# One encoder step on one core: seven products for eight in half of the second branch projection, and five modulation blocks summed on TensorE

## The chip, the cores and the metric

The kernel runs on one core of one Trainium2 chip. The metric is the device time of one execution in microseconds. Engines are named as in the profile: PE is TensorE's matmul, PEld its weight load, DVE is VectorE, ACT is ScalarE, POOL is GpSimd, SP is SyncE, which issues nearly all DMAs.

## The reference, cut to what matters

One layer is run for 512 prompt tokens and 64 sample tokens, 576 in all, with a model width of 1024. Two places of it are touched:

```python
mod = (silu(c) @ w_ada + b_ada)             # c: 1024; w_ada: 1024 x 6144, one row per stream
sh1, sc1, gt1, sh2, sc2, gt2 = split(mod, 6)
...
g_attn, g_ssm = split(sigmoid(gate_logits), 2)
mixed = (g_attn * (o_attn @ w_branch_attn) + g_ssm * (y @ w_branch_ssm)) @ w_out
x = x + gt1 * mixed
h2 = rms_normalize(x) * g_norm_ffn * (1 + sc2) + sh2
```

`o_attn` is 576 x 1024, `y` is 576 x 2048, `w_branch_attn` is 1024 x 1024 and `w_branch_ssm` 2048 x 1024. So the second branch projection contracts 16 tiles of 128 channels into 8 tiles of 128 output channels.

## The kernel before

All activations lie channel by channel: 128 channels on the partitions, 576 tokens along the row, and a matmul takes one half of the tokens, 288 columns. Every fp32 product is made of three fp32r matmuls: operands are split into a high part `h` (ACT copies with rounding) and a low part `l` (DVE subtracts), and hh, hl and lh are summed in PSUM. A weight tile is loaded by SP as `raw` (128 x 1024 elements, 512 KB, two buffers), ACT makes `wh` and DVE makes `wl` (three buffers each). `fetch` (line 612) and `getw` (line 641) issue these loads and splits in the order of a list `specs` of weight tiles. `fm` (line 926) makes one output tile: for each of its k tiles, three kinds of matmul times two token halves.

The order of instructions is fixed ahead of the run. The program records operations, and a planner (`Plan.order`, line 391) places them one engine at a time: whichever operation is ready by its own costs goes first, and among ready ones that with the lowest priority number, which is the place in the program less an offset set by `R.prio(...)` (4000 is urgent, -2000 is filler). `R.slack = 3.0` makes the planner place a matmul 3 us after its operands are due. At run time each engine runs its list in order and waits on semaphores only.

The stage in question, in order:

- The last state-space groups are finished beside the first branch projection. Eight tiles `fm(f"pba{a}", ...)` (line 1552) contract `oh`, `ol` (eight tiles each, pool `op_`, line 1316); the result times its gate goes to DRAM as `m_d`.
- `y`'s 16 tiles come from DRAM (`stage<-y_d`, two are kept in SBUF) and are split into `yh`, `yl` (line 1566, pool `yhl`, which opens once the state-space pool has closed).
- Five of the twelve blocks of 512 modulation values (u = 5 to 9; they hold `gt1`, `sh2` and `sc2`) are computed by `ada_columns` (line 770) as fillers: four 512 KB loads of `w_ada` each into two buffers `adr`, and on DVE sixteen multiply-adds of 128 x 512 into two accumulators `aacc`. `ada_sum` (line 787) then sums them over the partitions on PE: eight fp32 matmuls with 32 output rows each, four of them at four column positions of the array, and `ada_out` transposes the result.
- The second branch projection (line 1579): eight tiles of 16 x 3 x 2 matmuls, each then multiplied by its gate, added to `m` and split into `mh`, `ml`.
- The output projection with `w_out`, then the FFN, whose gate, up and down projections already take seven products for eight in part.

Two other ways of getting modulation values stand in the kernel: `ada_pair` at the start, which uses PE for the whole contraction, and `ada` (line 722), which is defined and not called.

Of the kernel before, what the change touches and what calls it, by code (L numbers as in the profile page):

```python
# [5 lines left out]
F32 = mybir.dt.float32  # L6
# [7 lines left out]
P = 128  # L14
# [526 lines left out]
def build(tc, I, O):  # L541
# [57 lines left out]
    queue = []  # L599
    state = {"ld": 0, "sp": 0, "get": 0}  # L600
    raws, outs, outs_made = {}, {}, []

    def fm_spec(w, c0, r0=0):
        specs.append([(kview(w[r0:r0 + 8 * P, c0:c0 + P]), 8, P)])
# [4 lines left out]
    def misc_spec():  # L609
        specs.append(["misc"])  # L610

    def fetch(done, limit=1 << 30):

        while len(outs_made) < len(specs):
            i = len(outs_made)
            outs_made.append(i)
            queue.extend((i, s) for s in specs[i])
            outs[i] = []
        with R.prio(4000 if done or limit > 99 else 0):
            more = True  # L620
            while more:
                more = False
                j = state["ld"]
                if j < min(len(queue), limit) and j < state["sp"] + NRAW:
                    i, s = queue[j]
                    if s == "misc":
                        raw = wp.tile([P, 8, 104], F32, name="rawm", tag="raw", bufs=NRAW)
                        sync.dma_start(raw[:, :, 0:72], kview(w_in[:, C_KI:C_KI + 72]))
                        sync.dma_start(raw[:, :, 72:104], kview(w_in[:, C_DT:C_DT + 32]))
                        raws[j] = (raw, 8, 104)  # L630
                    else:
                        raws[j] = (load_raw(*s), s[1], s[2], 27 <= j < 48)
                    state["ld"] += 1
                    more = True
                j = state["sp"]
                if j < min(state["ld"], limit) and (j < NWH or queue[j - NWH][0] < done):
                    outs[queue[j][0]].append(split(*raws.pop(j)))
                    state["sp"] += 1
                    more = True

    def getw(n=1):
        i = state["get"]
# [39 lines left out]
        nf += 1  # L682
    for a in range(8):
        fm_spec(I["w_branch_attn"][0], P * a)
    for a in range(8):
        fm_spec(I["w_branch_ssm"][0], P * a, 0)
        fm_spec(I["w_branch_ssm"][0], P * a, 1024)

    for a in range(8):
        fm_spec(I["w_out"][0], P * a)  # L690
# [28 lines left out]
    modc = cp.tile([P, 6, 8, 2], F32, name="modc")  # L719
    sh1, sc1, gt1, sh2, sc2, gt2 = (modc[:, i] for i in range(6))  # L720

    def ada(u, pl, bufs):

        p = px(f"pada{u}", "py")
        raws = [pl.tile([P, 2, 512], F32, name=f"wada{u}_{k2}", tag="adr", bufs=bufs) for k2 in range(4)]
        loads = [sync.dma_start(raw, w_ada[256 * k2:256 * k2 + 256, 512 * u:512 * u + 512].rearrange("(k p) n -> p k n", p=P))
                 for k2, raw in enumerate(raws)]
        with R.after(loads[-1:]):
            for kt in range(8):
                for g in range(4):  # L730
                    pe.matmul(p[32 * g:32 * g + 32, 0:P], sil[:, kt, :], raws[kt // 2][:, kt % 2, P * g:P * g + P],
                              start=(kt == 0), stop=(kt == 7), tile_position=(0, 32 * g))
        ada_out(u, p)

    pairs_bank = px("padp", "py")

# [33 lines left out]
    def ada_columns(u, pl, nacc=1, bufs=2, nk=2, tags=None, late=False):  # L770

        acc = [pl.tile([P, 512], F32, name=f"aacc{u}{s}", tag=tags[s] if tags else f"aacc{s}", bufs=nacc) for s in range(2)]
        for k0 in range(0, 8, nk):
            raw = pl.tile([P, nk, 512], F32, name=f"wada{u}_{k0}", tag=tags[2 + k0 // nk % 2] if tags else "adr", bufs=bufs)
            (pool if u == 10 else sync).dma_start(raw, w_ada[P * k0:P * (k0 + nk), 512 * u:512 * u + 512].rearrange("(k p) n -> p k n", p=P))
            for j in range(nk):
                kt = k0 + j
                for s in range(2):
                    if kt == 0:
                        vec.tensor_scalar(acc[s], raw[:, j], sil[:, kt, s:s + 1], None, op0=OP.mult)  # L780
                    else:
# [767 lines left out]

    t2 = lambda z: z.rearrange("p (a b) -> p a b", a=2)  # L1550
    m_d = R.dram([P, 8, T], F32, name="m_d")
    for a in range(8):
# [24 lines left out]
    ml = [mxp.tile([P, T], F32R, name=f"ml{k}") for k in range(8)]  # L1577
    mxt = R.mkpool("mixt", side="right", reuse_waits="tile")
    for a in range(8):
        g = mxt.tile([P, T], F32, name=f"gs{a}", tag="g", bufs=2)  # L1580
        sync.dma_start(g, gate_d[8 + a])
        m = mxt.tile([P, T], F32, name=f"m{a}", tag="m", bufs=2)
        sync.dma_start(m, m_d[:, a, :])
        ps = fm(f"pbs{a}", getw(2), lambda k: yh[k], lambda k: yl[k])
        vec.scalar_tensor_tensor(t2(g), t2(g), 1.0, ps, op0=OP.add, op1=OP.mult)
        vec.tensor_tensor(m, m, g, OP.add)
        for c0, n, d0, dn in ((0, NP_, 0, HP), (NP_, NS, HP, HS)):
            src = t2(m[:, c0:c0 + n])
            act.activation(t2(mh[a])[:, :, d0:d0 + dn], src, AF.Copy)
            vec.tensor_tensor(t2(ml[a])[:, :, d0:d0 + dn], src, t2(mh[a].bitcast(F32))[:, :, d0:d0 + dn], OP.subtract)  # L1590
    R.close(mxt, yh_p, adv, op_)


# [531 lines left out]
```

## Time and profile before

| | us |
|---|---|
| median of 3 runs (lowest, highest) | 1367.04 (1366.65, 1369.34) |
| the profiled execution's own time | 1366.41 |
| its span, first to last instruction | 1364.4 |
| PE busy in the span | 1346.8 (99%) |
| DVE busy | 1106.6 (81%) |
| ACT busy | 733.0 (54%) |
| POOL busy | 240.2 (18%) |

The device time is the span and about 2 us around it. All instructions pass through one helper, so every row of the profile names line 533, and rows are told apart by their tiles: `mm`, `px` and `py` are PSUM tiles, `yh,wl` is a matmul of those two operands, `aacc,pick` the sum over the partitions. A matmul's own duration (about 300 ns) overlaps its neighbours; what one costs is the distance from start to start. A fp32 matmul leaves two records, an fp32r matmul one.

### The profile page before, as it was taken

To read this page: it belongs to the slowest core of one execution; us is meant where nothing else is said; L and a number is where in the kernel's file an instruction comes from. 1 tells how busy PE (TensorE), PEld (TensorE's weight loads), DVE (VectorE), ACT (ScalarE), POOL (GpSimd) and SP (SyncE) were. 2 spreads that over 40 slices of the span, in tenths; PEclk is the share of its full clock that TensorE was granted. 3 is DMA by queue.
4 is the path that set the end of the run, shared out by engine and by line. 5 is a ranking of instruction groups with operands and counts; after the bars stand their busy time and mean duration, and the time that the engine had idled before them with its cause. 6 is when DMAs were issued, how large, how long until landed. Compare 5 with 4: busy or idle time off the path is not lost.

```text
span 1364.4 us, 27749 instructions
## 1 busy us (share of the span) xinstructions
PE 1346.8 (99%) x10699; PEld 1311.9 (96%) x10699; DVE 1106.6 (81%) x2237; ACT 733.0 (54%) x1535; POOL 240.2 (18%) x370
## 2 busy tenths in 40 slices
PE   7999999999999999999999999999999999999998
PEld 5999999999999999999999999999999999999998
DVE  5689998887778788888887599857899998878564
ACT  5445343776776766666675342225566665665221
POOL 1312002230310235545453200001000000000000
PEclk9999999999999999999999999999999999999999
DMA  9762435675754454454536698748233343325431
GB/s 298 227 178 84 109 104 140 142 164 126 179 140 116 137 168 118 117 153 122 150 96 193 209 316 241 224 147 257 73 109 94 109 124 94 93 77 156 123 107 36
DMA packets 267332, 199.52 MB, mean 146 GB/s; under 512 B 25152, under 2 KB 239328, under 8 KB 267200
## 3 DMA queue, kind: packets, MB, share of 16 engines
q1 hardware_dynamic: 263248, 183.59, 46.1%
q0 software_dynamic: 3952, 14.16, 5.2%
q8 instruction: 84, 1.38, 0.4%
q14 instruction: 48, 0.39, 0.1%
HBM read 157.75 MB, written 28.96 MB: 137 GB/s over the span
## 4 chain that ended last, share of the span: by engine, by line
PE 89%; DVE 6%; DMA 2%; issue 1%; SPq 1%; ACT 1%; POOL 0%; ACTq 0%; DVEq 0%; POOLq 0%
PE mm L533 64%; PE py L533 14%; PE px L533 11%; DVE score L533 1%; DMA raw<-in_w_in 1%; DVE m L533 1%; DVE wl L533 1%; SPq L533 1%; DMA xt<-in_x_sample 1%; DVE y L533 0%; DVE xlS L533 0%; DMA rawu<-in_w_gate_up 0%; DVE wh L533 0%; DVE tok L533 0%; DVE f L533 0%
## 5 line engine op out<-in xcount | busy, mean ns | idle before, releaser
L533 ACT ACTIVATE wh<-raw 128x1024 fp32r<-128x1024 f32 (+3 forms) x152 | 149.3, 984 | 209.0 <-PE mm L533 149.5
L533 PE MATMUL mm<-hTl,wh 128*128 128x288 f32 (+1 forms) x1024 | 231.9, 302 | 0.0
L533 PE MATMUL mm<-hTh,wh 128*128 128x288 f32 (+1 forms) x1024 | 231.7, 303 | 0.0
L533 PE MATMUL mm<-hTh,wl 128*128 128x288 f32 (+1 forms) x1024 | 230.7, 302 | 0.5 <-DVE wl L533 0.5
L533 PEld LDWEIGHTS mm<-hTh,wh 128*128 128x128 f32 (+1 forms) x1024 | 165.7, 189 | 3.6 <-issue 1.3
L533 PEld LDWEIGHTS mm<-hTl,wh 128*128 128x128 f32 (+1 forms) x1024 | 167.0, 189 | 1.8 <-issue 0.9
L533 PEld LDWEIGHTS mm<-hTh,wl 128*128 128x128 f32 (+1 forms) x1024 | 165.6, 189 | 2.5 <-issue 1.1
L533 DVE TENSOR_TENSOR wl<-raw,wh 128x1024 fp32r<-128x1024 f32 (+2 forms) x109 | 131.3, 1205 | 30.7 <-ACT wh L533 26.3
L533 DVE SCALAR_TENSOR_TENSOR cu<-xc,wc,cu 128x579 f32<-128x579 f32 x96 | 83.4, 869 | 2.0 <-ACT cu L533 1.0
L533 PE MATMUL mm<-wh,hTh 128*128 128x256 f32 x256 | 72.4, 285 | 0.0
L533 PE MATMUL mm<-wh,hTl 128*128 128x256 f32 x256 | 72.2, 284 | 0.0
L533 PE MATMUL mm<-wl,hTh 128*128 128x256 f32 x256 | 71.9, 282 | 0.0
L533 DVE SCALAR_TENSOR_TENSOR aacc<-adr,sil,aacc 128x512 f32<-128x512 f32 x84 | 58.7, 749 | 5.3 <-DMA adr<-in_w_ada 5.2
L533 PE MATMUL mm<-yh,wl 128*128 128x288 f32 x256 | 55.2, 296 | 0.0
L533 PE MATMUL mm<-yh,wh 128*128 128x288 f32 x256 | 55.0, 296 | 0.0
L533 PE MATMUL mm<-yl,wh 128*128 128x288 f32 x256 | 54.9, 296 | 0.0
L533 PE MATMUL mm<-xhS,wh 128*128 128x290 f32 (+1 forms) x248 | 54.8, 296 | 0.0
L533 ACT ACTIVATE P<-lg,mn 128x128 f32<-128x128 f32 (+4 forms) x72 | 41.7, 581 | 19.6 <-DVE mn L533 18.8
L533 PE MATMUL mm<-xhS,wl 128*128 128x290 f32 (+1 forms) x232 | 51.3, 296 | 0.0
L533 ACT ACTIVATE dec<-dec,nacs 128x128 f32<-128x128 f32 x128 | 42.4, 393 | 14.8 <-POOL dec L533 14.8
L533 PEld LDWEIGHTS mm<-wh,hTh 128*128 128x128 f32 x256 | 48.0, 188 | 0.5 <-issue 0.4
L533 PEld LDWEIGHTS mm<-wh,hTl 128*128 128x128 f32 x256 | 48.2, 189 | 0.2
(518 smaller groups left out, 3955.5 us busy)
## 6 DMA issues: line engine op xcount, KB each, us to landing
raw<-in_w_in SPq DMA_DIRECT2D x80, 512.0 KB, 4.3
adr<-in_w_ada SPq DMA_DIRECT2D x36, 512.0 KB, 4.8
raw<-in_w_gate_up SPq DMA_DIRECT2D x22, 512.0 KB, 3.9
wl<-raw POOLq DMA_DIRECT2D x21, 512.0 KB, 5.2
rawu<-in_w_gate_up SPq DMA_DIRECT2D x20, 512.0 KB, 4.0
bc<-acs_d SPq DMA_DIRECT2D x32, 256.0 KB, 3.4
raw<-in_w_branch_ssm SPq DMA_DIRECT2D x16, 512.0 KB, 4.5
raw<-in_w_down SPq DMA_DIRECT2D x16, 448.0 KB, 3.9
```

The source lines that it names most:

```text
L533: getattr(engines[x.eng], x.fn)(*[real(a) for a in x.args], **{k: real(v) for k, v in x.kw.items()})
```

## The change

The first eight of the 16 contracted tiles of the second branch projection go by Strassen's scheme in Winograd's form. Two output tiles, two groups of four k tiles and two token halves make a 2 x 2 by 2 x 2 product, done with seven products of four k tiles instead of eight, four times (r = 0 to 3). The other eight tiles are contracted as before. The seven weight operands of a pair are made on DVE out of two raw tiles (four subtractions of 128 x 512), which both stay in the two `raw` buffers until all seven are split; each split operand (`h` beside `l`) takes one slot of `wh` or `wl`, by turns. The seven operands of `y` are made from four loads of 128 x 4 x 288; three are kept in the pool of `y`, and four (S3, S1, A22, S4) in the buffers of `oh`, `ol`, which are free once the first branch projection has read them. Results are copied from PSUM into `acc0` and `acc1` and added there.

The five modulation blocks are no longer summed on DVE: `ada` does their whole contraction on PE with 32 fp32 matmuls of 32 output rows a block, straight from the loaded `w_ada`, which now has four buffers. They are placed by the planner 3 us after their loads are due, as urgent.

The diff, cut (the new weight order and the preparation of operands are left out where the text above says what they do):

```diff
+    def quad_source(key, pl, q):
+
+        b = pair_raws[key]
+        if "T2" not in b and q in ("T2", "T3"):
+            b["T1"], b["T3"] = b["B12"], b["B11"]
+            b["T2"] = pl.tile([P, 4, P], F32, name=f"T2b{key}", tag="T2b", bufs=1)
+            vec.tensor_tensor(b["T1"], b["B12"], b["B11"], OP.subtract)
+            vec.tensor_tensor(b["T2"], b["B22"], b["T1"], OP.subtract)
+            vec.tensor_tensor(b["T3"], b["T2"], b["B11"], OP.subtract)
+        if q == "T4":
+            b["T4"] = b["B21"]
+            vec.tensor_tensor(b["T4"], b["B21"], b["T2"], OP.subtract)
+        return b[q]
...
+                if j < min(len(preps), limit) and preps[j][2] <= state["ld"]:
+                    i, quad, n = preps[j]
+                    if quad is None and free("wh") and free("wl"):
+                        outs[i].append(split(*raws.pop(n - 1)))
+                        for tag in slots:
+                            slots[tag].append(i)
+                        state["sp"] += 1
+                        more = True
+                    tag = ("wh", "wl")[state["half"] % 2]
+                    if quad is not None and free(tag):
+                        r, q = quad
+                        if n - 2 in raws:
+                            x, y = (raws.pop(n - 2 + k)[0] for k in range(2))
+                            pair_raws[r] = {"B11": x[:, 0:4], "B21": x[:, 4:8], "B12": y[:, 0:4], "B22": y[:, 4:8]}
+                        src = quad_source(r, sum_pool[0], q)
+                        t = wp.tile([P, 8, P], F32R, name=f"wq{q}{r}", tag=tag, bufs=NWH)
+                        act.activation(t[:, 0:4], src, AF.Copy)
+                        vec.tensor_tensor(t[:, 4:8], src, t[:, 0:4].bitcast(F32), OP.subtract)
+                        outs[i].append((t[:, 0:4], t[:, 4:8]))
+                        slots[tag].append(i)
+                        state["half"] += 1
+                        state["sp"] += 1
+                        more = True
...
+    SSM_ORDER = (1, 2, 6, 7, 5, 4, 3)
+    SSM_QUADS = {1: ("B11", "A11"), 2: ("B21", "A12"), 6: ("T2", "S2"), 7: ("T3", "S3"), 5: ("T1", "S1"), 4: ("T4", "A22"), 3: ("B22", "S4")}
+    for r in range(4):
+        pair_spec(I["w_branch_ssm"][0], r, [SSM_QUADS[p][0] for p in SSM_ORDER])
+        for a in (2 * r, 2 * r + 1):
+            fm_spec(I["w_branch_ssm"][0], P * a, 1024)
...
-    def ada(u, pl, bufs):
+    def ada(u, raws):

         p = px(f"pada{u}", "py")
-        raws = [pl.tile([P, 2, 512], F32, name=f"wada{u}_{k2}", tag="adr", bufs=bufs) for k2 in range(4)]
...
+        with R.prio(4000):
+            R.slack = 3.0
+            with R.after(loads):
+                for kt in range(8):
+                    for g in range(4):
+                        pe.matmul(p[32 * g:32 * g + 32, 0:P], sil[:, kt, :], raws[kt // 2][:, kt % 2, P * g:P * g + P],
+                                  start=(kt == 0), stop=(kt == 7), tile_position=(0, 32 * g))
+            R.slack = SLACK
+            ada_out(u, p)
...
-    oh = [op_.tile([P, T], F32R, name=f"oh{k}") for k in range(8)]
-    ol = [op_.tile([P, T], F32R, name=f"ol{k}") for k in range(8)]
+    og = {n: [op_.tile([P, 4, T], F32R, name=f"o{n}{i}") for i in range(2)] for n in "hl"}
+    oh, ol = ([og[n][k // 4][:, k % 4, :] for k in range(8)] for n in "hl")
...
-    with R.prio(0):
-        for u in range(4 + NADX, 4 + NADX + NADA):
-            ada_columns(u, gtp, 2)
-    adv = R.mkpool("adav", reuse_waits="tile")
-    with R.prio(-2000):
-        for u in range(4 + NADX + NADA, 10):
-            ada_columns(u, adv)
     yh_p = R.mkpool("yhl", reuse_waits="tile")
-    yh = [yh_p.tile([P, T], F32R, name=f"yh{k}") for k in range(16)]
-    yl = [yh_p.tile([P, T], F32R, name=f"yl{k}") for k in range(16)]
-    for k in range(16):
+    yh, yl = ({k: yh_p.tile([P, T], F32R, name=f"y{n}{k}") for k in range(8, 16)} for n in "hl")
+    yq = {q: [yh_p.tile([P, 4, TH], F32R, name=f"y{n}{q}") for n in "hl"] for q in ("A11", "A12", "S2")}
+    src = {}
+    for i, q in enumerate(("A11", "A12", "A21", "A22")):
+        src[q] = gtp.tile([P, 4, TH], F32, name=f"yr{q}")
+        sync.dma_start(src[q], y_d[:, 4 * (i % 2):4 * (i % 2) + 4, TH * (i // 2):TH * (i // 2) + TH])
+
+    split_y("A11", src["A11"])
+    split_y("A12", src["A12"])
+    src["S2"] = gtp.tile([P, 4, TH], F32, name="yrS2")
+    vec.tensor_tensor(src["A21"], src["A11"], src["A21"], OP.subtract)
+    vec.tensor_tensor(src["S2"], src["A22"], src["A21"], OP.subtract)
+    split_y("S2", src["S2"])
+    vec.tensor_tensor(src["A12"], src["A12"], src["S2"], OP.subtract)
+    vec.tensor_tensor(src["A11"], src["A11"], src["S2"], OP.add)
+    for k in range(8, 16):
         if k < 14:
             load_split(gtp, y_d[:, k, :], yh[k], yl[k], 4)
         else:
             keep_split(ykeep[k - 14], yh[k], yl[k])
+    for q, v, o in (("S3", src["A21"], "h0"), ("S1", src["A11"], "l0"), ("A22", src["A22"], "h1"), ("S4", src["A12"], "l1")):
+        t = op_.tile([P, 2, 4, TH], F32R, name="y" + q, tag="o" + o)
+        yq[q] = [t[:, 0], t[:, 1]]
+        with R.prio(4000):
+            split_y(q, v)
     R.close(gtp)
+    with R.prio(-2000):
+        for u in range(4 + NADX, 10):
+            ada(u, [adv.tile([P, 2, 512], F32, name=f"wada{u}_{k2}", tag="adr", bufs=4) for k2 in range(4)])
...
+    for r in range(4):
+        for a in (2 * r, 2 * r + 1):
+            gates[a] = mxt.tile([P, T], F32, name=f"gs{a}", tag="g", bufs=2)
...
+        ps = pmm(f"pbs{r}")
+        bank = {"x": ps[:, 0, :TH], "y": ps[:, 1, :TH], "z": px(f"pbz{r}")[:, :TH]}
+        acc0 = adv.tile([P, T], F32, name=f"acc0{r}", tag="acc0", bufs=1)
+        acc1 = adv.tile([P, TH], F32, name=f"acc1{r}", tag="acc1", bufs=1)
+        for p in SSM_ORDER:
+            (hi, lo), = getw()
+            o, (yh_q, yl_q), starts = bank["y" if p == 2 else "z" if p in (7, 4) else "x"], yq[SSM_QUADS[p][1]], p in (1, 2, 7)
+            for k in range(4):
+                for w, y in ((hi, yh_q), (hi, yl_q), (lo, yh_q)):
+                    pe.matmul(o, w[:, k], y[:, k], start=(starts and k == 0 and w is hi and y is yh_q), stop=(k == 3 and w is lo),
+                              skip_group_check=not starts)
+            with R.prio(4000):
+                if p in (1, 6, 7):
+                    act.activation({1: acc0[:, :TH], 6: acc0[:, TH:], 7: acc1}[p], o, AF.Copy)
+                if p == 5:
+                    vec.tensor_tensor(acc1, acc1, o, OP.add)
+        (hi, lo), = getw()
+        for k in range(8):
+            for w, y in ((hi, yh), (hi, yl), (lo, yh)):
+                for hf, b in ((0, "y"), (1, "z")):
+                    pe.matmul(bank[b], w[:, k], y[8 + k][:, hf * TH:hf * TH + TH], start=False, stop=(k == 7 and w is lo), skip_group_check=True)
+        with R.prio(4000):
+            vec.tensor_tensor(acc0[:, :TH], acc0[:, :TH], bank["y"], OP.add)
+            vec.tensor_tensor(acc0[:, TH:], acc0[:, TH:], bank["z"], OP.add)
+        merged(2 * r, ((0, T, acc0),))
+        (hi, lo), = getw()
+        for hf, b in ((0, "x"), (1, "y")):
+            for k in range(8):
+                for w, y in ((hi, yh), (hi, yl), (lo, yh)):
+                    pe.matmul(bank[b], w[:, k], y[8 + k][:, hf * TH:hf * TH + TH], start=(hf == 1 and k == 0 and w is hi and y is yh),
+                              stop=(k == 7 and w is lo), skip_group_check=hf == 0)
+        with R.prio(4000):
+            vec.tensor_tensor(acc1, acc1, bank["y"], OP.add)
+        merged(2 * r + 1, ((0, TH, bank["x"]), (TH, TH, acc1)))
```

## Rows read from the trace of the kernel before

**Rows 1.** Windows of the span: busy us (records) of each engine, clock, DMA.
```profile
core 0: us, PE busy (x) PEld busy (x) DVE busy (x) ACT busy (x) POOL busy (x), PEclk, DMA share, GB/s
785.00:804.50 19.50, 19.50 (x149) 19.50 (x148) 18.73 (x28) 11.58 (x17) 0.00 (x0) 1.00 0.93 301
804.50:905.00 100.50, 100.50 (x813) 98.70 (x812) 84.11 (x133) 23.32 (x33) 0.31 (x3) 1.00 0.75 231
...
1007.00:1130.00 123.00, 123.00 (x920) 123.00 (x920) 121.97 (x232) 79.20 (x160) 0.00 (x0) 1.00 0.36 107
...
785.00:912.00 127.00, 127.00 (x1011) 125.19 (x1010) 104.73 (x163) 36.84 (x51) 2.17 (x10) 1.00 0.76 237
```

**Rows 2.** Groups on PE from 760 to 960 us: busy, mean ns of one, idle before.
```profile
L533 PE MATMUL mm<-yh,wl 128*128 128x288 f32 x256 | 55.2, 296 | 0.0
...
L533 PE MATMUL px<-aacc,pick 128*32 128x128 f32 x80 | 3.2, 279 | 0.0
```

**Rows 3.** Chain that ended last, 880 to 950 us and 1018 to 1034 us: start, us.
```profile
900.00 0.11 PE py L533
900.11 46.38 PE mm L533 x348
...
1021.49 4.83 PE mm L533 x36
```

**Rows 4.** Timeline of PE around one partition sum: start, us, records.
```profile
878.49 0.42 PE L533 MATMUL mm<-yl,wh 128*128 128x288 f32 x2
878.84 0.64 PE L533 MATMUL px<-aacc,pick 128*32 128x128 f32 x16
879.41 0.53 PE L533 MATMUL mm<-yh,wl 128*128 128x288 f32 x2
879.78 0.42 PE L533 MATMUL mm<-yh,wh 128*128 128x288 f32 x2
```

**Rows 5.** Timeline of PE in the start, where `ada_pair` contracts on PE.
```profile
32.06 1.07 PE L533 MATMUL py<-adr,sil 128*32 128x128 f32 x28
33.06 0.40 PE L533 MATMUL mm<-hTh,wh 128*128 128x288 f32 x1
```

**Rows 6.** The tile `adr`, whole span: its matmuls' records, durations min/median/max, forms.
```profile
L533 PE MATMUL py<-adr,sil x256: 272/273/423, 15.2 to 45.2; 128*32 128x128 f32 x128
```

**Rows 7.** Windows of the tile `aacc` alone: PE, PEld and DVE busy, clock.
```profile
785.00:912.00 127.00, 3.22 (x80) 1.88 (x80) 52.84 (x80) 1.00 0.76 237
```

**Rows 8.** Groups on DVE and ACT from 785 to 912 us: busy, mean ns, idle before.
```profile
L533 DVE TENSOR_TENSOR wl<-raw,wh 128x1024 fp32r<-128x1024 f32 x19 | 23.2, 1219 | 8.8 <-ACT wh L533 8.8
L533 DVE TENSOR_TENSOR yl<-stage,yh 128x576 fp32r<-128x576 f32 x14 | 10.0, 751 | 0.7 <-ACT yh L533 0.7
...
L533 ACT ACTIVATE wh<-raw 128x1024 fp32r<-128x1024 f32 x20 | 21.2, 1059 | 76.6 <-PE mm L533 52.3 <-issue 21.6 <-DMA raw<-in_w_branch_ssm 2.8
```

**Rows 9.** Groups on DVE and ACT from 1007 to 1130 us, the FFN's products.
```profile
L533 DVE TENSOR_TENSOR wh<-T,wh 128x512 fp32r<-128x512 f32 x23 | 15.7, 685 | 0.0
...
L533 DVE TENSOR_TENSOR gg<-t,px 128x290 f32<-128x290 f32 x11 | 5.0, 451 | 0.1
...
L533 ACT ACTIVATE wh<-T 128x512 fp32r<-128x512 f32 x22 | 13.7, 624 | 2.2 <-PE px L533 2.2
...
L533 ACT ACTIVATE t<-mm 128x290 f32<-128x290 f32 x11 | 4.5, 414 | 7.1 <-PE mm L533 7.1
```

**Rows 10.** Loads of `raw`, then of `adr`, from 780 to 905 us: issue to landing.
```profile
DMA to landing us min/median/max: 4.2/4.5/6.4
...
DMA to landing us min/median/max: 3.7/4.5/6.6
```

**Rows 11.** Timelines of DVE and PE where the first branch projection ends.
```profile
798.68 0.76 DVE L533 SCALAR_TENSOR_TENSOR g<-g,mm 128x576 f32<-128x576 f32 x1
...
804.88 0.42 PE L533 MATMUL mm<-yh,wh 128*128 128x288 f32 x2
...
911.33 0.75 DVE L533 SCALAR_TENSOR_TENSOR g<-g,mm 128x576 f32<-128x576 f32 x1 [4.03 <-PE mm L533]
```

More of the change, by code (lines that the diff above doesn't have):

```diff
@@ L598, in build @@
     specs = []
-    queue = []
-    state = {"ld": 0, "sp": 0, "get": 0}
-    raws, outs, outs_made = {}, {}, []
+    loads, preps = [], []
+    state = {"ld": 0, "sp": 0, "get": 0, "half": 0}
+    raws, outs, outs_made, slots, pair_raws = {}, {}, [], {"wh": [], "wl": []}, {}
     def fm_spec(w, c0, r0=0):
@@ L610, in misc_spec, with pair_spec @@
         specs.append(["misc"])
+    def pair_spec(w, r, names):
+        for i, q in enumerate(names):
+            specs.append([("quad", w, r, q, i == 0)])
+    def quad_source(key, pl, q):
[10 more added lines that the diff above has]
+        return b[q]
+    sum_pool = []
     def fetch(done, limit=1 << 30):
@@ L616, in fetch @@
             outs_made.append(i)
-            queue.extend((i, s) for s in specs[i])
             outs[i] = []
+            for x in specs[i]:
+                if x[0] == "quad":
+                    _, w, r, q, first = x
+                    if first:
+                        for c in (2 * r, 2 * r + 1):
+                            loads.append([(kview(w[0:8 * P, c * P:c * P + P]), 8, P), 0])
+                    for l in loads[-2:]:
+                        l[1] = len(preps)
+                    preps.append((i, (r, q), len(loads)))
+                else:
+                    loads.append([x, len(preps)])
+                    preps.append((i, None, len(loads)))
         with R.prio(4000 if done or limit > 99 else 0):
@@ L623, in fetch @@
                 j = state["ld"]
-                if j < min(len(queue), limit) and j < state["sp"] + NRAW:
-                    i, s = queue[j]
-                    if s == "misc":
+                if j < min(len(loads), limit) and (j < NRAW or loads[j - NRAW][1] < state["sp"]):
+                    x = loads[j][0]
+                    if x == "misc":
                         raw = wp.tile([P, 8, 104], F32, name="rawm", tag="raw", bufs=NRAW)
@@ L631, in fetch @@
                     else:
-                        raws[j] = (load_raw(*s), s[1], s[2], 27 <= j < 48)
+                        raws[j] = (load_raw(*x), x[1], x[2], 27 <= j < 48)
                     state["ld"] += 1
@@ L635, in fetch @@
                 j = state["sp"]
[L636 to L639, printed above, removed]
+                free = lambda tag: len(slots[tag]) < NWH or slots[tag][-NWH] < done
+                if j < min(len(preps), limit) and preps[j][2] <= state["ld"]:
[21 more added lines that the diff above has]
+                        more = True
     def getw(n=1):
@@ L684, in build @@
         fm_spec(I["w_branch_attn"][0], P * a)
-    for a in range(8):
-        fm_spec(I["w_branch_ssm"][0], P * a, 0)
-        fm_spec(I["w_branch_ssm"][0], P * a, 1024)
+    SSM_ORDER = (1, 2, 6, 7, 5, 4, 3)
[4 more added lines that the diff above has]
+            fm_spec(I["w_branch_ssm"][0], P * a, 1024)
     for a in range(8):
@@ L720, in build @@
     sh1, sc1, gt1, sh2, sc2, gt2 = (modc[:, i] for i in range(6))
-    def ada(u, pl, bufs):
+    def ada(u, raws):
         p = px(f"pada{u}", "py")
-        raws = [pl.tile([P, 2, 512], F32, name=f"wada{u}_{k2}", tag="adr", bufs=bufs) for k2 in range(4)]
         loads = [sync.dma_start(raw, w_ada[256 * k2:256 * k2 + 256, 512 * u:512 * u + 512].rearrange("(k p) n -> p k n", p=P))
                  for k2, raw in enumerate(raws)]
[L728 to L733, printed above, removed]
+        with R.prio(4000):
[7 more added lines that the diff above has]
+            ada_out(u, p)
     pairs_bank = px("padp", "py")
@@ L1551, in build @@
     m_d = R.dram([P, 8, T], F32, name="m_d")
+    adv = R.mkpool("adav", reuse_waits="tile")
+    sum_pool.append(adv)
     for a in range(8):
@@ L1558, in build, with split_y @@
             sync.dma_start(m_d[:, a, :], g)
-    with R.prio(0):
-        for u in range(4 + NADX, 4 + NADX + NADA):
-            ada_columns(u, gtp, 2)
-    adv = R.mkpool("adav", reuse_waits="tile")
-    with R.prio(-2000):
-        for u in range(4 + NADX + NADA, 10):
-            ada_columns(u, adv)
-    yh_p = R.mkpool("yhl", reuse_waits="tile")
-    yh = [yh_p.tile([P, T], F32R, name=f"yh{k}") for k in range(16)]
-    yl = [yh_p.tile([P, T], F32R, name=f"yl{k}") for k in range(16)]
-    for k in range(16):
+    yh_p = R.mkpool("yhl", reuse_waits="tile")
+    yh, yl = ({k: yh_p.tile([P, T], F32R, name=f"y{n}{k}") for k in range(8, 16)} for n in "hl")
[4 more added lines that the diff above has]
+        sync.dma_start(src[q], y_d[:, 4 * (i % 2):4 * (i % 2) + 4, TH * (i // 2):TH * (i // 2) + TH])
+    def split_y(q, v):
+        keep_split(v, *yq[q])
+    split_y("A11", src["A11"])
[7 more added lines that the diff above has]
+    for k in range(8, 16):
         if k < 14:
@@ L1578, in build, with merged @@
     mxt = R.mkpool("mixt", side="right", reuse_waits="tile")
[L1579 to L1585, printed above, removed]
+    def merged(a, parts):
+        g, m = gates[a], mixed[a]
+        for c0, n, ps in parts:
+            vec.scalar_tensor_tensor(g[:, c0:c0 + n], g[:, c0:c0 + n], 1.0, ps, op0=OP.add, op1=OP.mult)
         vec.tensor_tensor(m, m, g, OP.add)
@@ L1590, in build @@
             vec.tensor_tensor(t2(ml[a])[:, :, d0:d0 + dn], src, t2(mh[a].bitcast(F32))[:, :, d0:d0 + dn], OP.subtract)
+    gates, mixed = {}, {}
+    for r in range(4):
+        for a in (2 * r, 2 * r + 1):
+            gates[a] = mxt.tile([P, T], F32, name=f"gs{a}", tag="g", bufs=2)
+            sync.dma_start(gates[a], gate_d[8 + a])
+            mixed[a] = mxt.tile([P, T], F32, name=f"m{a}", tag="m", bufs=2)
+            sync.dma_start(mixed[a], m_d[:, a, :])
+        ps = pmm(f"pbs{r}")
[32 more added lines that the diff above has]
+        merged(2 * r + 1, ((0, TH, bank["x"]), (TH, TH, acc1)))
```

## The prediction

> **What bounds the kernel now.** I read the windows first. From 785 to 912 us, from the last state-space work to the end of the second branch projection, PE is busy 127.00 of 127.00 us at full granted clock, DVE 104.73 and ACT 36.84 [rows 1]. So the stage is bound by PE, with DVE near its limit in its first part (18.73 of 19.50 us) and in the FFN (121.97 of 123) [rows 1]. The groups on PE then say whether it waited: each of the three kinds of matmul of the projection has no idle time before it [rows 2]. A matmul's own 296 ns is no price, since neighbours overlap; the chain of waits has the price: 348 matmuls of 288 columns in 46.38 us, 133.3 ns each [rows 3]. That explains the stage whole: 768 matmuls are 102.4 us, from 804.88 to the last gate product at 911.33 are 106.5 us [rows 11], and five partition sums with their transposes, 0.87 us each (below), are the other 4. No hidden hole is left to fill. In a stage like this each matmul removed is worth its 133 ns and each one added is paid in full, whoever had done that work before.
>
> **What the change removes from PE.** Per pair of output tiles there were 2 x 16 x 3 x 2 = 192 matmuls. Now there are seven products of 4 x 3 = 84, and for the other eight contracted tiles 2 x 8 x 3 x 2 = 96: 180. Four pairs save 48 matmuls, 48 x 133.3 ns = 6.40 us. That a product keeps this rate, twelve matmuls into one PSUM bank, is shown by the FFN: 36 matmuls of its products, of 288 or 290 columns, take 4.83 us, 134 ns each [rows 3], and its window of 123 us holds 920 matmuls, 133.7 ns each, with PE never idle [rows 1].
>
> **What it adds on PE.** A modulation block was 8 fp32 matmuls of 32 output rows, 16 records; there are 80 records for five blocks [rows 2]. It becomes 32 matmuls. At the start of the kernel the same form leaves 256 records for 128 matmuls [rows 6], so a block has 64 records. Their price: 28 of them run from 32.06 to the next matmul at 33.06, 1.00 us, 35.7 ns each (such a run stands four times in the start) [rows 5]; and in this very stage 16 run from 878.84 to 879.41, 35.6 ns each [rows 4]. The rest of a block stays: from 878.49 to 879.78 are 1.29 us, of which 0.57 are the records and 4 x 0.133 the four matmuls beside them, so 0.19 us go at its two ends; the transpose is 0.11 us [rows 3, 4]. The old block is 0.87 us, the new one 64 x 35.7 + 190 + 110 ns = 2.58 us. Five times the difference of 48 records is 5 x 48 x 35.7 ns = 8.57 us.
>
> PE's work thus grows by 8.57 - 6.40 = 2.17 us, and PE is what bounds the stage. This is the firmest term.
>
> **What it takes from DVE buys nothing by itself.** The multiply-adds of the five blocks, 80 operations and 52.84 us of busy DVE [rows 7], go away. PE waited for none of them. In their place come: 16 subtractions for weight sums and 28 low halves of 128 x 512 at 0.685 us [rows 9], less 8 full low halves at 1.219 [rows 8], +20.4 us; seven low halves and four sums of `y` operands of 1152 columns, estimated from 1.219 us for 1024 as 1.37 us, less eight low halves at 0.751, +9.1 us [rows 8]; four additions of 288 columns per pair at 0.45 [rows 9], +7.2 us, and a split gate product, +0.6. DVE ends about 15 us lighter. ACT gets 28 half conversions at 0.624 for 8 full ones at 1.059, +9.0 us, seven of 1152 columns (estimated 1.19 us) for eight of 576, about +3 us, and twelve copies of 0.41, +5 us, on 37 of 127 [rows 1, 8, 9]: covered. The bytes moved stay the same, so DMA's 0.75 share does too [rows 1].
>
> **The waits it adds.** Inside a pair the products share banks: x is copied out after products 1 and 6 before it is added to again, z after 7, x is read by DVE after 5. One product of 12 matmuls, 1.6 us, lies between; a copy is 0.41 and an addition 0.45 us [rows 9]. The FFN has the same spacing and loses nothing [rows 1]. I take 0. The upper bound: an operation of 1.22 us [rows 8] just begun, 0.45 us and two hand-offs of 0.2 us exceed 1.6 us by 0.5 us, 2 us over four pairs. Behind such a wait all of PE's queue stands.
>
> The hand-over from the first branch projection is tighter. A22 and S4 take buffers that the first projection reads to its end, at 804.88 [rows 11]; so do the weight slots of T1 and T4. By program order ACT then makes two conversions of 1.19 us and two of 0.62: it is done at 805.1 + 3.6 = 808.7. DVE follows with two of 1.37 and two of 0.685, from 806.3 to 810.4. The products need these operands between 811 and 815 and get them. But only then is one raw buffer free, and the plain weights of the pair can be loaded: 4.5 us median [rows 10], so 815.0; 1.06 us on ACT, 1.22 on DVE [rows 8], low half at 817.4. The seven products end at 804.88 + 84 x 0.133 = 816.1, and the first matmul with a low half is the fifth, at 816.6. PE stands 0.8 us, by the median load. By the slowest load, 6.4 us, it is 2.7 us; it is 0 if a modulation block (2.58 us) falls between, and below nothing it cannot be, since PE had no idle time here to give back. I take 0.8, the value of the median row. In later pairs the slots of T1 and T4 come free at the pair's start, with nothing of `y` in the queue: by the same steps the low half is there about 9.5 us after it, and it is needed at 11.7. I take 0, with the slowest load too.
>
> DVE in this hand-over, from 785.8 to 816.1, has about 31 us of work for 30 (seven low halves and four sums of `y`, 15; seven half weights, four sums and two full ones, 10; gate products and `y`'s first three plain tiles, 6), where it was full before too. `y`'s remaining plain tiles are wanted 0.8 us apart, each 0.75 us on DVE, so this costs up to 1 us more; I leave it in the range.
>
> The modulation blocks themselves wait for four loads each. Each fills its four buffers only after the block before has been read, and while its matmuls wait, everything on PE waits behind them. They are placed 3 us after they are due. The loads of `adr` took 4.5 us in the median and 6.6 at most [rows 10]: 2.1 us of scatter against 3. I take 0; the bound is 2.1 us for each of five blocks, 10.5 us. Loads of quarters of `y`, the larger tiles for `oh`, the later opening of the gate buffers cost nothing: they lie beside the first projection, with `yh` split 15 us before it is wanted; without that cover a load of 5 us would stand on PE.
>
> **The sum.** +2.17 + 0.8 = +3.0 us. On the profiled execution's 1366.4 us (span 1364.4 and 2.0 around it) this is 1369.4. That execution lies 0.6 us below the median of the runs shown, 1367.04; on the median it is 1370.0, and that I give. 0.2%, about what a measurement can tell from no change, is 2.7 us.
>
> **The rivals.**
> *The work alone.* A modulation block falls into the hand-over, or the load comes early, and PE never stands: +2.2 us, 1369.2, within 0.2%. For it speaks that some block is due about every 13 us (loads, 3 us, 2.6 us of PE).
> *Late plain weights in every pair.* Two raw buffers hold a pair until its last operand is split, and a load delayed in SP's queue behind modulation loads comes 2 us late each time: 4 x 1.9 (6.4 instead of 4.5 us) + 2.2 = +9.8, 1376.8. Against it: 2 us of slack in three of four pairs.
> *Modulation loads late.* Five blocks, each 2.1 us: +12.7, 1379.7. Half of it is likelier than all.
> *Faster, by packing.* Four column positions of the array could work beside each other. If the added 240 records cost less than 6.40 us / 240 = 26.7 ns each, the change wins; below 15.3 ns it wins over 0.2%. At 128 of 290 columns of a 134 ns matmul, a pass is 59 ns, and four side by side in two passes would be 118 ns for 8 records, 14.7 ns each: 3.5 - 6.4 = -2.9 us, 1364.1. Against it stand two rows at 35.7 and 35.6 ns, both at full clock [rows 4, 5]. The Trainium skill says that such packing is up to four times as fast (TensorEngine Tiling, Theoretical Speedup); by that rule the change would gain, and the trace does not agree: eight records take 286 ns, not 118.
> *Holes filled.* If the new blocks fell into holes of PE, 6.4 us would remain as gain, 1360.6. PE's 127.00 of 127 us [rows 1] speaks against it.
>
> **How the numbers follow.** Hand-over wait, as forecast: 0.42, itself 1369 to 1372, two in three of it beyond 0.2%. Work alone: 0.28, one in ten of it beyond. Late plain weights 0.12, late modulation loads 0.10, packing 0.05, holes 0.03. Slower: 0.27 + 0.03 + 0.22 = 0.52. Faster: 0.08. The rest, 0.40, is the same. The range from 1367.5 to 1376 leaves out the two faster cases and about half of the two late ones, some 0.19.
>
> **What would show it.** 64 records a block, 320 in all, 2.3 us from first to last; 720 fp32r matmuls for the projection where 768 stood; from its first matmul to its last gate product 109 us or a little more instead of 106.5. A wait of PE for a low half near 816 shows the hand-over; waits for `adr` or a low half later show the rivals. The forecast is wrong if a block's records take under 27 ns each, if PE's waits pass 3 us, or if PE had idle time that the blocks use.

## The result, and the profile after

| | before | after |
|---|---|---|
| median (lowest, highest), us | 1366.85 (1365.24, 1369.34), 6 runs | 1381.01 (1379.52, 1385.15), 6 runs |
| profiled execution, span, us | 1366.41, 1364.4 | 1380.62, 1378.6 |

The ratio is 1.011, interval 1.0092 to 1.0128: 14 us slower, outside the predicted range of 1367.5 to 1376. The direction was the forecast's; the size and, as it turned out, the reason were not.

The same two windows as [rows 1], of after. The columns are length, then busy us (records) of PE, PEld, DVE, ACT and POOL, PE's clock, DMA share and GB/s.

```profile
785.00:804.50 19.50, 18.36 (x139) 18.23 (x140) 15.60 (x23) 10.89 (x17) 2.38 (x1) 1.00 0.86 278
804.50:905.00 100.50, 94.06 (x931) 89.59 (x930) 65.28 (x109) 33.63 (x58) 0.00 (x0) 1.00 0.66 206
```

PE, which was busy for the whole of both windows before, now stands for 1.1 and 6.4 us of them, while DVE and ACT have room (65 and 34 of 100.5 us). So PE isn't slower: it waits. The stage, from the last matmul of the projection before it to the first with `mh` (the output projection), took 172.4 us before and takes 186.7: +14.3, all of the difference. These rows mark its ends after (timeline of PE; start, us, engine, records):

```profile
739.45 0.43 PE L533 MATMUL mm<-hTh,wl 128*128 128x288 f32 x2
...
926.24 0.43 PE L533 MATMUL mm<-mh,wh 128*128 128x288 f32 x2
```

For whom PE waited there, from the view of waits (735 to 930 us; the columns are total us, times, longest; the same view of before names no wait):

```profile
PE px L533 <- DVE r L533: 2.4, 1, 2.4
PE mm L533 <- DVE g L533: 2.2, 4, 0.5
PE mm L533 <- DVE acc L533: 2.0, 4, 0.5
PE mm L533 <- ACT acc L533: 2.0, 4, 0.5
PE py L533 <- DVE ra L533: 1.3, 1, 1.3
PE py L533 <- DVE xwS L533: 0.2, 1, 0.2
```

Twelve waits of 0.5 us stand there, three kinds by four: one set for each pair of output tiles. The timeline shows what the first of them is. PE, at the end of the second product, which goes into `y`:

```profile
813.54 0.43 PE L533 MATMUL mm<-yhA,wl 128*128 128x288 f32 x2
813.80 0.29 PE L533 MATMUL mm<-ylA,wl 128*128 128x288 f32 x1
814.60 0.40 PE L533 MATMUL mm<-yhA,wl 128*128 128x288 f32 x1 [0.50 <-ACT acc L533]
814.84 0.56 PE L533 MATMUL px<-oh,wl 128*128 128x288 f32 x3
```

and ACT, which copies `x` out:

```profile
814.13 0.41 ACT L533 ACTIVATE acc<-mm 128x288 f32<-128x288 f32 x1 [2.27 <-PE mm L533]
```

The first product, into `x`, ended at 812.5. Yet the copy of `x` starts only when PE's matmul into `y` from 813.80 is done, and PE's next matmul into `y` starts only when the copy is done. The two have nothing in common but the tile: `x` and `y` are the two banks of one tile, `ps = pmm(...)`, and the waits are kept by tile. The planner counts by bank, and so saw nothing. From 813.80 to 814.84 are 1.04 us for two matmuls of 0.133, so one such wait costs 0.77 us, with its hand-offs and the slower start behind it; twelve are 9.3 us.

The other two waits come from DVE's order. Here is DVE before the one of 2.4 us:

```profile
781.12 0.41 DVE L533 COPY rowsZ<-px 128x128 f32<-128x128 f32 x2
784.59 1.36 DVE L533 TENSOR_TENSOR yrA<-yrA,yrA 128x1152 f32<-128x1152 f32 x1 [3.06 <-DMA yrA<-y_d]
785.87 0.21 DVE L533 TENSOR_SCALAR r<-px 128x4 f32<-128x4 f32 x2
```

DVE was free from 781.5, but its list had the first sum of `y` next, whose load had not landed (the quarters took 8.1 us in the median). The small operation `r` behind it, 0.2 us long, is what PE needed, at 783.6, 0.13 us behind the start of its last matmul (783.45). In the same way `ra`, the copy that a block's transpose needs, was late at 826.78 behind two low halves whose weights had come late. Loads landed later altogether than the rows of before say: from 780 to 905 us those of `raw` took 5.6 us in the median and 7.9 at most, those of `adr` 6.6 and 7.7, where [rows 10] have 4.5 and 6.4, 4.5 and 6.6.

Finally the block itself, timeline of PE:

```profile
806.99 1.95 PE L533 MATMUL py<-adr,sil 128*32 128x128 f32 x64
808.87 0.40 PE L533 MATMUL mm<-oh,wl 128*128 128x288 f32 x1
```

64 records from start to start in 1.88 us. The old block's 16 took 0.57 [rows 4]. So 48 records more cost 1.31 us, 27.3 ns each, and five blocks 6.55 us.

### The profile page after: what moved, and what is told of

Read it like the earlier page. It is cut to its first block, busy times and chain, and to the rows that moved or that the text cites. A ratio compares the mean times of both kernels' runs of the same rounds, so it can differ in the third digit from the quotient of the medians.

```text
span 1378.6 us, 28120 instructions
## 1 busy us (share of the span) xinstructions
PE 1351.9 (98%) x10891; PEld 1313.3 (95%) x10891; DVE 1092.9 (79%) x2216; ACT 747.5 (54%) x1566; POOL 244.2 (18%) x370
## 4 chain that ended last, share of the span: by engine, by line
PE 88%; DVE 6%; DMA 3%; issue 1%; SPq 1%; ACT 1%; POOL 1%; ACTq 0%; DVEq 0%; POOLq 0%
PE mm L533 60%; PE py L533 16%; PE px L533 12%; DVE score L533 1%; DVE m L533 1%; DVE wl L533 1%; SPq L533 1%; DMA yrA<-y_d 1%; DMA xt<-in_x_sample 1%; DMA adr<-in_w_ada 1%; DMA raw<-in_w_branch_ssm 0%; DVE g L533 0%; DMA bc<-acs_d 0%; DVE tok L533 0%; DVE yrA L533 0%
## 5 line engine op out<-in xcount | busy, mean ns | idle before, releaser
L533 DVE TENSOR_TENSOR wl<-raw,wh 128x1024 fp32r<-128x1024 f32 (+2 forms) x101 | 122.9, 1218 | 33.1 <-ACT wh L533 30.5
L533 PEld LDWEIGHTS mm<-wl,hTh 128*128 128x128 f32 x256 | 48.1, 188 | 0.3
L533 PE MATMUL mm<-fh,wh 128*128 128x288 f32 x224 | 48.2, 296 | 0.0
L533 PE MATMUL mm<-fh,wl 128*128 128x288 f32 x224 | 47.9, 296 | 0.0
L533 PE MATMUL mm<-fl,wh 128*128 128x288 f32 x224 | 47.7, 296 | 0.0
```

What stands on the lines that cost most here:

```text
L533: getattr(engines[x.eng], x.fn)(*[real(a) for a in x.args], **{k: real(v) for k, v in x.kw.items()})
```

## The experiments

Five theories. **A**: the twelve waits come from two banks in one tile. **B**: they come from the spacing of the products, wherever the results lie. **C**: the other waits come from small operations of DVE that PE needs and that stand, in DVE's fixed order, close behind operations with late data; distance in the plan cures them. **D**: DVE is too full; a wait moved away comes back elsewhere. **E**: in versions with blocks on DVE, it is the fewer buffers. Median times are given with the ratio to before on the same chip (1367.51 us for the first four runs, 1367.8 for the next four, 1367.57 for the last three).

**One part each: the tile, and the blocks.** e1_own_tile gives `y` a PSUM tile of its own:

```diff
-        bank = {"x": ps[:, 0, :TH], "y": ps[:, 1, :TH], "z": px(f"pbz{r}")[:, :TH]}
+        bank = {"x": ps[:, 0, :TH], "y": px(f"pby{r}")[:, :TH], "z": px(f"pbz{r}")[:, :TH]}
```

> The changed kernel with one edit: result bank y of a pair gets a PSUM tile of its own (tag px) instead of the second bank of the tile that holds x. Theory A (waits are kept by tile: x and y are two banks of one tile, so a copy out of x waits for matmuls into y that were issued before it, and the next matmul into y waits for that copy; three times a pair, twelve in all, about 0.8 us each): the twelve waits go, 9.5 us faster than the changed kernel, about 1371.5, still 4 to 5 us over the kernel before. Rival B (one product is too short a distance, and the copies are late by themselves): the same twelve waits stand, 1380 to 1382.

Measured 1375.45 us, ratio 1.0058 [1.0037, 1.008]; the stage is 179.85 us long. Its waits of PE in the stage, whole list:

```profile
PE px L533 <- DVE r L533: 2.3, 1, 2.3
PE py L533 <- DVE ra L533: 1.9, 3, 0.9
PE px L533 <- ACT acc L533: 0.2, 1, 0.2
```

All twelve are gone: A. Less came back than twelve waits cost, since three transposes now wait for `ra`, and for a second reason, in the windows around the wait for `r`:

```profile
784.90:787.30 2.40, 0.20 (x2) 0.00 (x0) 1.47 (x3) 0.00 (x0) 0.00 (x0) 1.00 1.08 382
787.90:791.10 3.20, 3.20 (x16) 3.20 (x14) 0.84 (x1) 0.10 (x1) 1.87 (x1) 0.50 0.70 187
791.10:797.00 5.90, 5.90 (x46) 5.89 (x46) 3.59 (x6) 1.90 (x3) 0.00 (x0) 0.98 0.84 271
```

Behind the wait the granted clock fell to 0.50, the lower of its two levels (1.2 GHz), and 14 matmuls stand 240 ns apart instead of 133: 1.5 us more.

e2_z_beside_x moves `z` into the tile of `x` instead, so that other pairs of products share a tile:

```diff
-        bank = {"x": ps[:, 0, :TH], "y": ps[:, 1, :TH], "z": px(f"pbz{r}")[:, :TH]}
+        bank = {"x": ps[:, 0, :TH], "y": px(f"pby{r}")[:, :TH], "z": ps[:, 1, :TH]}
```

> The changed kernel with y in a tile of its own, but z as the second bank of x's tile. The same banks are copied at the same points, only the partner in the tile is another. Theory A: no wait in the second product any more, but new ones in the products into z and x that lie between a copy and its matmuls (third, fourth, sixth) and in the first plain tile, three or four a pair: 1380 to 1385, as slow as the changed kernel or slower. Rival B: where a bank lies makes no difference: the same places and 1380 to 1382. If only the number of PSUM tiles mattered: 1371.5, as with y alone.

Measured 1385.25 us, 1.0134 [1.0117, 1.015]. The waits for `acc` in the stage, and two of them on the timeline:

```profile
PE mm L533 <- DVE acc L533: 6.6, 8, 2.5
PE mm L533 <- ACT acc L533: 4.7, 8, 1.1
```

```profile
819.66 0.93 PE L533 MATMUL mm<-oh,wl 128*128 128x288 f32 x5 [0.50 <-ACT acc L533]
820.43 0.43 PE L533 MATMUL mm<-ol,wh 128*128 128x288 f32 x2
821.36 1.59 PE L533 MATMUL mm<-ol,wh 128*128 128x288 f32 x10 [0.50 <-ACT acc L533]
```

Same products, same spacing, same order: the waits are sixteen. In each pair they stand in products 7, 5 and 4, the fourth, fifth and sixth in order (the expectation had the third, fourth and sixth), and in a plain tile, where PE writes one of `x` and `z` while the other is read, and none stands in product 2. A holds, B falls.

e3_blocks_only makes the kernel before do the five blocks on PE, without the seven products (one buffer for `m` less, for room):

```diff
-            ada_columns(u, adv)
+            ada(u, [adv.tile([P, 2, 512], F32, name=f"wada{u}_{k2}", tag="adr", bufs=4) for k2 in range(4)])
```

> The kernel before with the five modulation blocks on PE and nothing else of the change (the tile of m in the gate product has one buffer instead of two, for room). By the prediction's price of 35.7 ns a record: +8.6 us, 1375.4. By what the changed kernel's own blocks show (2.07 us each beside a transpose, where the old ones took 0.76): +6.6 us, 1373.4. If the blocks cost waits as well (a transpose behind a late DVE, loads late): 1 to 2 us more.

Measured 1374.15 us, 1.0049 [1.0034, 1.0064]: +6.6 us. There is no wait of PE in the stage:

```profile
785.00:918.00 133.00, 133.00 (x1245) 131.19 (x1244) 57.05 (x83) 36.34 (x51) 0.51 (x1) 1.00 0.70 225
...
829.50 1.96 PE L533 MATMUL py<-adr,sil 128*32 128x128 f32 x64
831.38 0.40 PE L533 MATMUL mm<-yh,wl 128*128 128x288 f32 x1
```

A block again takes 1.88 us, so 6.55 us for the five is their price by the timeline, and the rise of the median, 6.6 us, lies next to it. The rise alone would not decide: its interval, 4.6 to 8.8 us, takes in the prediction's 8.57. That PE waits for nothing here also says that DVE's lighter load (57 us of 133) was worth nothing there.

**The other waits.** e4_sums_later is e1 with the first sum of `y` placed on DVE behind the two kept tiles of `y`:

```diff
-    vec.tensor_tensor(src["A21"], src["A11"], src["A21"], OP.subtract)
+    with R.after([o for y in ykeep for _, o in y.base.writes]):
+        vec.tensor_tensor(src["A21"], src["A11"], src["A21"], OP.subtract)
```

> As the kernel with y in its own tile, and the first sum over y's quarters (A11 - A21) is placed behind the last gate products of the state-space part instead of in the first gap of DVE. Theory C (DVE stood 3.1 us in its order before that sum, for a load that landed late, and a small operation behind it kept PE for 2.4 us): PE's wait at 786 goes, 2.5 us faster than the kernel with y in its own tile, about 1369. Rival D (PE would have waited there for another thing, or the time comes back in the hand-over to the second projection): the same as the kernel with y in its own tile, within 1 us.

Measured 1374.92 us, 1.005 [1.0035, 1.0065]. The wait for `r` is gone, the waits for `ra` have grown from 1.9 to 5.2 us, and one for `wl` has come:

```profile
PE py L533 <- DVE ra L533: 5.2, 2, 3.2
PE px L533 <- DVE wl L533: 0.5, 1, 0.5
```

By its time this is D, though some 3 us of it are the lower clock behind the two waits for `ra` (last section). But these two are again a transpose behind a DVE that has other work before `ra`, so C could still be right with distance there. e5_transpose_slack is e4 and that:

```diff
+        R.slack = 3.0
         pe.transpose(p2[:, 0:P], ra, ident)
+        R.slack = SLACK
```

> As the kernel with the later sum, and each modulation block's transpose is placed 3 us after DVE's copy is due. In that kernel PE waited 5.6 us, twice, for this copy, which stood in DVE's order behind a weight split whose load had landed late. Theory C (every such wait is an in-order DVE that stands for a late load, and PE stands only where a matmul was placed right behind it): the two waits go, 1374.9 - 5.6 = 1369.5. Rival D (DVE is late altogether, and PE meets the lateness at the next operand): 1373 to 1375, with waits for weight halves or operands in their place.

Measured 1369.56 us, 1.0018 [1.0009, 1.0027], the stage 176.2 us: C's time. Six waits are left, 2.0 us in all by the view of waits. e8_loads_due_later is another way to the same, e1 with SP's loads of the stage entered in the plan as 3 us later:

```diff
-                op.t1 = dma_free + op.dur_dma
+                op.t1 = dma_free + op.dur_dma + op.late
...
+    R.late = 3.0
```

> The kernel with y in its own tile, where the planner takes every load that SP issues from the first branch projection to the end of the second as due 3 us later; nothing else is changed. Theory C: the operations that wait for loads are placed later, nothing else stands behind them in DVE's order, and what PE waited for in that kernel (2.4 us at the last gate of the state space, 2.4 at three transposes, 0.3) goes: 1375.4 - 5 = 1370.5, before and the blocks' price aside nothing is left. Rival D: work placed later is missed later, 1374 to 1378.

Measured 1374.55 us, 1.0057 [1.0035, 1.0078]. The wait for `r` went, and one of 4.8 us came, with the lower clock behind it:

```profile
PE py L535 <- DVE ra L535: 4.8, 1, 4.8
```

```profile
813.70:817.50 3.80, 3.71 (x17) 3.72 (x18) 3.80 (x7) 1.75 (x5) 0.00 (x0) 0.56 0.43 113
```

As in e4, one measure alone moves the wait to the transpose. Later transposes alone were not tried. e9_loads_and_transpose joins e8's late loads and e5's transposes; e10_all_three has the later sum as well.

> The kernel with y in a tile of its own, SP's loads of the stage counted as 3 us later, and the transposes of the blocks placed 3 us after they are due. Loads later alone left one wait of 5.1 us (a transpose for DVE's copy ra) and took 1374.55 us. If PE's order only lacked distance to DVE (theory C), that wait goes too: 1374.5 - 5 = 1369.5 us, the stage 174.5 us long where it was 179.3. If the time comes back at another place whatever is moved (rival D), 1373 to 1375 us, with waits of 2 us or more elsewhere in the stage.

> The same, and the first sum of y on DVE is placed behind the two tiles of y that are kept. With transposes and sum moved but the loads as planned the time was 1369.56 us, with 2.9 us of waits left in six places. Theory C: the later loads take one to two of these away, 1368 us (1367.3 to 1369.5), no more than the work's +0.15 us and the ends of five blocks away from before. Rival D: no better than 1369.6, the waits only move.

Measured: e9 1366.85 us, ratio 1.0 [0.9992, 1.0009]; e10 1365.72 us, 0.9992 [0.9983, 1.0001]. Both are better than C's numbers (1369.5 and 1368), and D falls: in e10 the waits don't come back when the loads, the transposes and the sum all have distance. e10's only wait of PE in the stage, and its windows, as in [rows 1]:

```profile
PE mm L535 <- DVE acc L535: 0.5, 1, 0.5
```

```profile
804.50:905.00 100.50, 100.01 (x995) 97.96 (x994) 63.20 (x110) 36.60 (x62) 0.00 (x0) 1.00 0.72 223
785.00:912.00 127.00, 126.51 (x1194) 124.46 (x1193) 87.00 (x140) 49.73 (x81) 0.00 (x0) 1.00 0.71 220
```

PE is as full as it was before, and the stage takes 173.5 us against 172.4. So the change without its waits is worth nothing that can be told from no change. e9's profiled execution was 2.7 us above e9's median. It holds a wait of 2.6 us, for `ra`, and the lower clock behind it:

```profile
PE py L535 <- DVE ra L535: 2.6, 1, 2.6
```

```profile
814.20:817.10 2.90, 2.82 (x12) 2.83 (x13) 2.90 (x3) 0.54 (x2) 0.00 (x0) 0.50 0.53 150
```

Three of e9's eleven executions lie at 1369.6 to 1370.5 us and eight at 1366.0 to 1367.5; whether the faster ones lack that wait was not seen.

**Was moving the blocks to PE needed?** e6_sums_on_dve is e5 with all five blocks back on DVE, e7_two_on_dve with two, e11_one_on_dve with one; e7 and e11 have a buffer less each for gates, `m` and `ra`, for room, and load `m` later; in all three the sums of DVE's blocks lie in another PSUM tile (`py`).

```diff
-            ada(u, [adv.tile([P, 2, 512], F32, name=f"wada{u}_{k2}", tag="adr", bufs=4) for k2 in range(4)])
+            ada_columns(u, adv)
```

> As the kernel with the later sum and the later transposes, but the five modulation blocks are summed on DVE as before the change; only the seven products are left of the change, with y in its own tile. If PE's work alone decides: 48 matmuls fewer, 6.4 us under the kernel before, 1361. If DVE bounds it: DVE has about 104.7 + 37 = 142 us of work in a stage of 121 us of PE, the last blocks come 10 us late or more, and PE waits in the output projection for its gate and scale: 1365 to 1375.

> The same with three modulation blocks on PE and the last two (u = 8, 9) on DVE; for room the gate tiles of the first projection have three buffers instead of four, m and the transposes' copies one instead of two. PE's work: -6.4 + 3 x 1.31 = -2.5 us, 1365.0, if nothing waits; DVE then has about 110 us of work in 124. If late loads still hold DVE and DVE holds PE: 2 to 5 us more, 1367 to 1370.

> The kernel of the 1369.56 us (own tile, later sum, transposes 3 us later) with the last of the five blocks (u = 9) summed on DVE as before the change, and one buffer less for gates, one for m and one for ra, which makes room. By the price of a record PE has 48 x 27 ns = 1.3 us less to do: 1368.3 us if DVE and the smaller buffers lose nothing. Two blocks on DVE gave 1374.3, with PE waiting for loads, ACT and gates. If the smaller buffers did that (rival E), it is 1371 to 1374 here too; if DVE's load did it (theory D), half of it, 1370 to 1371.

Measured: e6 1386.13 us, 1.0135 [1.0114, 1.0156]; e7 1374.29, 1.0047 [1.003, 1.0064]; e11 1372.31, 1.0045 [1.0028, 1.0062]. e6 and e7 are slower than either of their expectations. In e6 DVE is the bound: it is busy 139 of the 152 us up to 937, and PE stands 11.5 us for its last sum, at 936.68.

```profile
785.00:937.00 152.00, 132.64 (x1023) 128.36 (x1022) 138.83 (x221) 51.55 (x84) 5.51 (x10) 0.97 0.67 207
```

```profile
PE py L533 <- DVE aacc L533: 11.5, 1, 11.5
PE py L533 <- DVE ra L533: 2.2, 1, 2.2
```

So as planned here the seven products can't have five blocks on DVE beside them. e7's and e11's longest waits tell more of the third question. Of e7, then of e11:

```profile
PE py L533 <- DMA adr<-in_w_ada: 2.2, 2, 1.3
PE px L533 <- ACT acc L533: 1.9, 1, 1.9
PE mm L533 <- DVE acc L533: 1.1, 1, 1.1
```

```profile
PE mm L533 <- DVE acc L533: 2.0, 2, 1.1
PE py L533 <- DMA adr<-in_w_ada: 1.6, 2, 1.3
```

The two can't be told apart: 2.0 us lie between the medians, but the ratios are alike and the executions overlap (1371.3 to 1376.6 us, and 1370.3 to 1378.0). e11's is rival E's time (1371 to 1374). For the waits for `adr` the traces point to the gates' buffer. From 780 to 793 us, ahead of the first loads of `adr`, SP waited for a gate product to be written to `m_d`, so that the next gate could be loaded into its buffer, in e5 and then in e7:

```profile
SPq L533 <- DMA m_d<-g: 5.8, 1, 5.8
SPq L533 <- DMA m_d<-g: 10.1, 2, 6.0
```

The first load of `adr` went at 789.31 us in e5, at 791.52 in e7 and, behind two such waits of 9.6 us together, at 792.97 in e11. What the waits for `acc` come from was not tried, and DVE's part isn't excluded.

## Why the prediction was wrong

**The step that failed is "The waits it adds":** "The FFN has the same spacing and loses nothing [rows 1]. I take 0", with 2 us as the upper bound over four pairs. It cost 9.3 us, and PE's waits in the stage, 10.1 us by the view of waits, are past the 3 us that the prediction named as a sign against itself. The comparison looked at the spacing of the products and not at the tiles: in the FFN's seven products `x` is alone in its `mm` tile and `y` and `z` lie in `px` and `py`; here `x` and `y` are halves of one. The bound had the wrong mechanism too: it let an engine be late by half a microsecond, where here both engines stop for each other however early they are. Both were to be read in the diff, in the line that e1 changes. The Trainium skill (PSUM — Partial Sum Buffer, PSUM bank collisions raise a hardware error) asks for semaphores by bank and quadrant; that a wait by bank would do here is what e1 shows, with a tile for each bank.

**"What it takes from DVE buys nothing by itself"** held (e3). But that DVE ended lighter was taken to mean that it would not be late. The prediction weighed DVE's sum of work and not what stands next in its list: two waits, 2.4 and 1.3 us, behind late loads. "Loads of quarters of `y` ... cost nothing" named the cover of `yh` only, and not the sums behind these loads nor the small operations behind the sums.

**"What it adds on PE"** was mis-sized, and it was called the firmest term: 35.7 ns a record against 27.3, 8.57 against 6.55 us. A run's length from its first record to the next matmul holds the change of tile at its ends as well, which the prediction added again as 0.19 us. From runs of 16 and 64 records (0.57 and 1.88 us) the ends come out at 0.13 us. A run also has a grain. Windows of the tile `adr` in after, at the start of a block, PE alone (start and end, length, busy us, records under way, clock, DMA):

```profile
806.98:807.02 0.04, 0.03 (x4) 1.00 0.00 0
807.02:807.11 0.09, 0.09 (x4) 1.00 0.00 0
807.13:807.16 0.03, 0.03 (x8) 1.00 0.00 0
```

Four records start within 0.03 us, then none for about 0.1 us, then four more: a group of four costs 4 x 27.3 = 109 ns. The kernel issues its four column positions one behind the other, so this looks like the packing of the prediction's rival, four records for the 0.11 us that the one record of the transpose takes [rows 3]; which record belongs to which position the trace doesn't show. The 28 records of [rows 5] are six groups of four and two of two (24 have started by 32.66, 26 by 32.77, 28 by 32.88): eight groups of 109 ns and the ends are 1.00 us, as measured. The Trainium skill (TensorE: Matmul & The Clock Gate, Wait — 56ns, not 53.3ns?) says that matmuls never start less than about 25 ns apart, however small. The trace does not agree for these records: four start within 0.03 us.

**"What the change removes from PE"**, 48 matmuls and 6.40 us, is borne out: e10 does seven products and five blocks on PE in 1.2 us more of the stage, by 6.55 - 6.40 = +0.15, one wait of 0.5 and 0.5 that are not placed. So the work adds about 0.15 us, not 2.17.

The account of +14.3 us: work +0.15, twelve waits 9.3 (the one that was read, times twelve), the two behind DVE 3.7 by the view of waits; 1.1 us are not placed.

**The hand-over** didn't wait: no low half was late at 816, a block stood ahead of it at 806.99, as the text allowed for. **The rivals:** no wait for `adr` in after, so the modulation loads were in time, though they took 6.6 us in the median and not 4.5; late plain weights showed only through `ra`, once; packing showed in kind, by the groups of four, but at 27.3 ns a record it just missed its break-even of 26.7 and gained nothing; there were no holes. The prediction gave packing 0.05 and set 286 ns for eight records against it: that is the pace with the ends in it, and without them eight records take 218 ns. Its own estimate of 118 ns went wrong at the pass, which it scaled to 59 ns from the fp32r matmuls of 290 columns; a group of four fp32 records takes 109. "Work alone" is what e9 and e10 reach, at less than its price, and not what after did. None of the rivals was the mechanism that decided, and the range's upper end rested on two that didn't occur.

Not settled: e10's median lies 1.85 us below before's while its profiled stage is 1.2 us longer; its interval takes in no change. The two profiled executions also differ far from the stage: from 24 to 28 us the mean granted clock was 0.57 in before and 1.00 in e10.

## What to carry to other kernels

When two results that are read and written at different times lie in two banks, give each a tile of its own, or check by what unit the waits are kept: a planner that counts by bank doesn't see waits that are kept by tile. Where PE has no idle time, ask of every small operation that it waits for what stands ahead of it in its engine's list and whether that waits for a load; an engine's busy share doesn't tell. Price short records by the difference of two runs of different length, not by one run over its count, and look whether they start in groups.

## What was not expected of the hardware

A wait of PE can cost more than its length. Behind waits of 2.3 us (e1) and 2.6 us (e9) the granted clock was 0.50 for about 3 us, some 1.5 us lost each. Behind the one of 2.4 us in after it did not fall:

```profile
786.10:790.00 3.90, 3.87 (x30) 3.74 (x31) 2.07 (x3) 1.33 (x2) 2.38 (x1) 1.00 0.75 210
```

So the same wait at the same place cost 1.5 us more in one kernel than in the other. The other runs are as mixed: the clock was 0.50 behind the two waits of e4 for `ra` (2.1 and 3.2 us), and in e11 behind two waits for `adr` of 1.6 us together, but not in e7 behind two of 2.2 us at the same place. So the length of a wait alone doesn't decide it, and what does was not tried.
